# A two-layer hybrid backbone: modulation products between the layers, one indirect transfer per 128 rows, second experts by columns

## Chip, cores and metric

The kernel runs on one core of a Trainium2 chip, as one program. The metric is the device time of one execution in microseconds, the median over runs.

## The reference, cut to what matters

A latent stream (256 tokens) and a context stream (256 tokens), 1,024 wide, pass through two layers. Each layer takes six modulation rows from a product of the conditioning vector with `w_ada`; a mixer works on the normalized, modulated streams, and then a mixture of 16 experts, of which each token uses two out of one group of four. Layer 0's mixer is windowed attention beside a gated recurrence, layer 1's a gated scan beside Fourier mixing. In layer 1 only the latent stream goes on, so its experts see 256 tokens and layer 0's 512.

```python
for l in range(DEPTH):
    need_ctx = l < DEPTH - 1
    mod = (jax.nn.silu(c) @ w_ada[l] + b_ada[l])[:, None, :]
    mod_c = (jax.nn.silu(c_ctx) @ w_ada[l] + b_ada[l])[None, None, :]
    sh1, sc1, g1, sh2, sc2, g2 = jnp.split(mod, 6, axis=-1)
    ...
    h = layer_norm_affine(DEEPNORM_ALPHA * h + g1 * m, ln_g[l, 0], ln_b[l, 0])
    u = modulate(layer_norm(h), sh2, sc2)
    ...
    h = layer_norm_affine(DEEPNORM_ALPHA * h + g2 * y, ln_g[l, 1], ln_b[l, 1])

def moe(t, w_router, b_router, w1, w3, w2):
    ...
    for e in range(N_EXPERTS):
        h = jax.nn.silu(t @ w1[e]) * (t @ w3[e])
        y = y + gates[:, e:e + 1] * (h @ w2[e])
```

## The kernel before

The program runs in five stages: `mixer0` (from L631), `moe` for layer 0 (L1451 on, with `l == 0`), `mixer1` (L1083), `moe` for layer 1, and a tail (L1918 on) with the last norm. Within a stage a planner lays out each engine's order ahead of time from estimated durations, and it interleaves steps of neighbouring experts; where `in_order` (L149) is called, the order written in the code holds for the engines named. The second `moe` calls it for PE, ACT and DVE.

Precision: a product in the mixers is made of three passes over fp32r halves. `split` (L351) makes a high half by a copy on ACT (L353) and a low half by a subtraction on DVE (L355); `split_w` (L359) does it for a weight, with one buffer for the low half `wl`. The experts' products are plain fp32.

Modulation: `w_ada` comes in 12 column parts `j` of 512 per layer. `ada_load` (L244) fetches one as two tiles of 1 MB, `ada_part` (L248) does 16 matmuls with it (L254). `ada_row` (L271) adds the bias row, which it fetches into the one tile `bz` on POOL's queue (L274), and broadcasts the result over the partitions for either stream (L281); `ada_col` (L260) copies it on ACT (L262) and transposes it into columns with eight small matmuls (L265). In `mixer0` a generator `fill0` (L656) hands these steps out one by one between the projections' weights and the heads of the recurrence: rows 4 to 11 of layer 0, then eight column parts of layer 1.

Experts: `Ring` (L1421) hands out weight tiles of 1 MB from a round of slots in three pools, among them the slots `m` of `rp` and `w` of `wp`, which the mixers use for other things; six tiles make an expert, loaded on SP (L1441). `load_more` asks for tiles ahead. An expert takes its tokens in units: `cni` holds, per expert, the count in units of 32 rows, and branches (`tc.If`) on it leave out what isn't needed. In `moe` of layer 0 the tokens' rows are gathered from DRAM by indirect transfers on POOL, 64 rows each, and results scattered to `y_d` likewise (L1508). `up` (L1581, L1585) makes both up products of 64 rows in 32 matmuls, `mid` the gating on ACT and DVE (L1598, L1599), `hpose` transposes (L1605, copied on DVE at L1607), `down` (L1610, L1613) takes 16 matmuls.

In `moe` of layer 1 the rows are picked on PE: `select` (L1512, DVE) makes a one-hot matrix, `rows` (L1520, L1525) multiplies it with the normalized stream, ACT copies (L1534, L1567), `rows_T` transposes (L1541) and modulates on DVE and ACT. Experts with at most 32 rows take `up32` (L1588, L1593) and `down32` (L1617, L1621), which work on four column groups of 32 rows. `weigh` (L1817) gates the output on ACT and splits it in two halves; `seat` (L1717) makes the transposed selection, and `add` (L1730, L1735) adds the expert's rows into four accumulators of PSUM.

`large` (L1827) comes after the experts: a conditional pass over those with more rows than the main loop holds; it loads their tiles through the same ring and isn't entered with these inputs. In `mixer1`, `y_load` (L1119) fetches the experts' two results of a block of 128 tokens into a tile `yk` of the slots `m` (L1122), `block` (L1125) combines them with the residual, norms and transposes; the blocks of the latent stream (2, 3) come first and the gate's projection weights (`cols_w`, L1099, slots `w`) follow them.

The ring's slots, as the code gives them:

```python
ring.slots += [lambda sh, dt: wx.tile(sh, dt, name="wx", tag="w", bufs=nx)] * nx
ring.slots += [lambda sh, dt: rp.tile(sh, dt, name="wm", tag="m", bufs=2)] * 2
ring.slots += [lambda sh, dt: wp.tile(sh, dt, name="w", tag="w")] * NW
```

## Time and profile before

| | us |
|---|---|
| median of 3 runs | 1491.35 (1484.99 to 1494.71) |
| profiled execution, device time | 1492.23 |
| its span | 1490.4 |
| mean granted PE clock | 0.917 of full speed |
| first mixer | 0 to about 515 |
| first experts | 521 to 846 |
| from the last product of the experts to the first of the second mixer | 846 to 894 |
| second mixer and router | 894 to 1162 |
| second experts | 1162 to 1468 |
| tail | 1468 to 1490 |

The rows below come from one profiled execution. PE is the matmul engine, PEld its weight loads, DVE, ACT and POOL the vector, scalar and general engines, SPq the queue of the engine that issues most transfers. A row of the timeline gives the start, the length, the engine, the line in the kernel, the operation with its tiles (output <- inputs), the shape and the count; in brackets stands how long the engine sat idle before and what released it. Lines are those of the kernel before.

### The profile page before, as it was taken

What the parts mean: (1) busy time and instruction counts of PE and PEld (TensorE: products, weight loads), DVE (VectorE), ACT (ScalarE), POOL (GpSimd) and SP (SyncE); (2) the same over time, 40 slices, a digit from 0 to 9 for tenths busy, and PEclk for the clock granted to TensorE, in tenths of its full rate; (3) what the DMA queues carried; (4) which work ended last, traced back from release to release, by engine and by line L of the source; (5) the groups of instructions that cost most, each with busy time, mean ns of one, the idle gap of its engine ahead of it and who ended that gap; (6) DMA issues with size and microseconds to landing.
All of it is one profiled execution on the core that took longest, in us unless ns stands there. A gap on an engine that the chain in (4) does not pass through costs nothing. (4 is left out here: it accounts for less than half of the span.)

```text
span 1490.4 us, 20670 instructions
## 1 busy us (share of the span) xinstructions
PE 1231.3 (83%) x7920; PEld 753.5 (51%) x7920; DVE 663.0 (44%) x1615; ACT 412.9 (28%) x849; POOL 101.0 (7%) x135
## 2 busy tenths in 40 slices
PE   4899999988879399999999607999976787888883
PEld 2667887555659233333333207887556244444441
DVE  4432323575767712221112167645647244444444
ACT  2323223354534011111111023451231333323222
POOL 1000000110020211111101000000010000000000
PEclk9899999998969699999999857999977899999996
DMA  8465564700011799999977052421466699979831
GB/s 286 173 225 172 200 225 170 214 13 1 1 52 62 264 338 377 363 355 372 344 285 253 21 170 88 127 63 58 156 240 246 255 344 346 368 273 326 325 128 59
DMA packets 152248, 310.69 MB, mean 208 GB/s; under 512 B 7596, under 2 KB 39660, under 8 KB 152088
## 3 DMA queue, kind: packets, MB, share of 16 engines
q1 hardware_dynamic: 146320, 296.44, 56.5%
q0 software_dynamic: 4608, 8.59, 2.1%
q10 hardware_dynamic: 1160, 3.48, 0.6%
q8 instruction: 105, 1.72, 0.5%
q14 instruction: 55, 0.45, 0.1%
HBM read 303.24 MB, written 9.44 MB: 210 GB/s over the span
## 5 line engine op out<-in xcount | busy, mean ns | idle before, releaser
L372 PE MATMUL mm<-wh,uT 128*128 128x256 f32 (+2 forms) x960 | 193.7, 297 | 7.4 <-ACT uT L353 4.8
L372 PEld LDWEIGHTS mm<-wh,uT 128*128 128x128 f32 x960 | 159.0, 198 | 20.6 <-issue 9.0
L372 PE MATMUL mm<-wl,uT 128*128 128x256 f32 (+2 forms) x480 | 141.7, 296 | 4.2 <-DVE wl L355 4.2
L1585 PE MATMUL mm<-wx,xT 128*64 128x512 f32 x504 | 143.1, 600 | 1.6 <-PEq L1753 0.8
L372 PEld LDWEIGHTS mm<-wl,uT 128*128 128x128 f32 x480 | 95.0, 198 | 5.8 <-DVE wl L355 5.3
L355 DVE TENSOR_TENSOR wl<-w,wh 128x2048 fp32r<-128x2048 f32 (+3 forms) x33 | 53.8, 1646 | 71.4 <-ACT wh L353 54.2
L1599 DVE TENSOR_TENSOR hs<-hs,mm 64x512 f32<-64x512 f32 x32 | 22.1, 691 | 127.5 <-ACT hs L1598 81.3
L1585 PEld LDWEIGHTS mm<-wx,xT 128*64 128x64 f32 x504 | 44.6, 138 | 66.3 <-issue 64.5
L254 PE MATMUL mm<-w,sT 128*32 128x512 f32 x384 | 61.3, 644 | 10.9 <-DVE v L298 9.1
L353 ACT CAST wh<-w 128x2048 fp32r<-128x2048 f32 (+3 forms) x33 | 45.8, 1388 | 67.2 <-DMA w<-in_w_in_even_dram 53.3
L372 PE MATMUL mm<-uT,wh 128*128 128x512 f32 (+1 forms) x208 | 59.0, 370 | 4.9 <-ACT wh L353 4.9
L1598 ACT ACTIVATE hs<-mm 64x512 f32<-64x512 f32 x32 | 18.8, 589 | 147.0 <-PE mm L1585 97.2
L372 PE MATMUL mm<-wo,mx 128*128 128x256 f32 x384 | 52.4, 296 | 5.3 <-ACT wo L353 3.5
L1613 PE MATMUL mm<-wx,hT 128*64 128x512 f32 x192 | 54.1, 597 | 1.7 <-PEq L1796 0.9
L372 PEld LDWEIGHTS mm<-wo,mx 128*128 128x128 f32 x384 | 49.6, 202 | 6.0 <-ACT wo L353 3.8
L1585 PE MATMUL mm<-w,xT 128*64 128x512 f32 x120 | 47.0, 596 | 0.3 <-PEq L1753 0.2
L1639 DVE COPY ys<-mm 64x512 f32<-64x512 f32 x22 | 15.2, 693 | 67.6 <-ACT ys L1639 64.4
L372 PEld LDWEIGHTS mm<-uT,wh 128*128 128x128 f32 (+1 forms) x208 | 36.4, 184 | 14.0 <-ACT wh L353 5.2
L1585 PE MATMUL tr<-wx,xT 128*64 128x512 f32 x152 | 39.1, 595 | 3.2 <-PE ac L1541 2.8
L1525 PE MATMUL ac<-h,sel 128*64 128x512 f32 x104 | 28.0, 660 | 16.4 <-DVE sel L1516 16.4
L1148 PE MATMUL tr<-cst,yk 128*128 128x128 f32 x32 | 5.4, 324 | 43.4 <-ACT yk L1141 43.4
L372 PE MATMUL mm<-uT,wl 128*128 128x512 f32 (+1 forms) x104 | 37.7, 366 | 2.3 <-DVE wl L355 2.3
(468 smaller groups left out, 2304.5 us busy)
## 6 DMA issues: line engine op xcount, KB each, us to landing
w<-in_w_ada_dram SPq DMA_DIRECT2D x48, 1024.0 KB, 6.0
wx<-in_w_expert_gate_dram SPq DMA_DIRECT2D x46, 1024.0 KB, 9.3
wx<-in_w_expert_up_dram SPq DMA_DIRECT2D x44, 1024.0 KB, 8.4
wx<-in_w_expert_down_dram SPq DMA_DIRECT2D x39, 1024.0 KB, 9.0
w<-in_w_expert_down_dram SPq DMA_DIRECT2D x15, 1024.0 KB, 7.8
w<-in_w_in_even_dram SPq DMA_DIRECT2D x13, 1024.0 KB, 10.4
w<-in_w_expert_up_dram SPq DMA_DIRECT2D x12, 1024.0 KB, 8.3
wm<-in_w_expert_down_dram SPq DMA_DIRECT2D x10, 1024.0 KB
```

The source lines that it names most:

```text
L254: nc.tensor.matmul(ps[32 * g:32 * g + 32, :], sT[:, k, :], ws[k // 4][:, k % 4, :], start=k < 4, stop=k >= 4, skip_group_check=True, tile_ ...
L353: nc.scalar.copy(hi, src)
L355: nc.vector.tensor_tensor(lo, src, hi.bitcast(FP), op=OP.subtract)
L372: nc.tensor.matmul(ps, lhs(i, k), rhs(j, k), start=(k == 0 and n == 0), stop=(k == nk - 1 and n == 2))
L1148: nc.tensor.transpose(ps[:, k * 128:(k + 1) * 128], y[:, kk_ * 128:(kk_ + 1) * 128], ident)
L1525: nc.tensor.matmul(xp[i * 64:i * 64 + 64, :], sel[:, b, :], u[:, i * 512:(i + 1) * 512], start=b == 0, stop=b == len(us) - 1, skip_group_c ...
L1585: nc.tensor.matmul(hp[i * 64:i * 64 + 64, :], xT[:, k, :], ws[2 * i + k // 4][:, k % 4, :], start=k == 0, stop=k == 7, skip_group_check=Tr ...
L1598: nc.scalar.activation(hs, hp[0:64, :], AF.Silu)
L1599: nc.vector.tensor_tensor(hs, hs, hp[64:128, :], op=OP.mult)
L1613: nc.tensor.matmul(yp[n * 64:n * 64 + 64, :], hT[:, k, :], ws[4 + k // 2][:, k % 2, n * 512:(n + 1) * 512], start=k == 0, stop=k == 3, ski ...
L1639: (nc.vector.tensor_copy if n else nc.scalar.copy)(ys[:, ns], yp[rs_, :])
```

## The change

The row parts 10 and 11 of layer 0's modulation (`g2`) and the eight column parts of layer 1 leave `fill0`; they are made at the end of the first experts, ahead of `large`, and their tiles come through the ring. In the first experts one indirect transfer handles 128 rows, and the router writes its lists in that form with plain fp32 products. In the second mixer the first gate weight is asked for ahead of the latent blocks, whose y loads are issued by POOL and whose order on DVE and ACT is pinned; the two streams lie in two tiles. `moe` becomes `moe0` and `moe1`. `moe1` takes the normalized stream as two fp32r halves and makes the transposed rows of a group of four experts at once (`group`, `half_group`, `columns`), modulated as they leave PSUM; the forms for 32 rows are gone, a second unit of 64 rows has its own conditional path (`unit_up`, `unit_down`), the output is gated and scaled in one operation (`row_out`), and an add serves two experts. Its ring has 15 slots for 16.

The diff, cut:

```diff
+    def ada_load(l, j, ring=None):
         src = w_ada[l][:, j * 512:(j + 1) * 512]
-        return [load_w(src[q * 512:(q + 1) * 512, :], 4, 512) for q in range(2)], (l, j)
+        ws = []
+        for q in range(2):
+            w = ring.tile([128, 4, 512]) if ring else wp.tile([128, 4, 512], FP, name="w", tag="w")
+            nc.sync.dma_start(w, src[q * 512:(q + 1) * 512, :].rearrange("(k p) n -> p k n", p=128))
+            ws.append(w)
+        return ws, (l, j)
...
+    def ada_row(l, j, dsts, add1=0.0, col=False, ld=None):
+
+        ld = ld or ada_load(l, j)
...
-                self.io = cp.tile([64, 2, 16 * NU], I32, name="io")
+                self.io = cp.tile([128, 2, 8 * NU], I32, name="io")
...
-            for i in range(2):
-                nc.tensor.matmul(self.tps[0:64, 0:16 * NU], R[:, i], Cm[:, i].rearrange("p e j -> p (e j)"),
-                                 start=n == 0 and i == 0, stop=last and i == 1, skip_group_check=True)
+
+            for o in range(2):
+                for i in range(2):
+                    nc.tensor.matmul(self.tps[o * 64:o * 64 + 64, 0:8 * NU], R[:, i],
+                                     Cm[:, i].rearrange("p e j -> p (e j)")[:, o::2], start=n == 0 and i == 0,
+                                     stop=last and i == 1, skip_group_check=True, tile_position=(0, o * 64))
...
-            for j, t, add1 in ((4, g1, 0.0), (5, g1, 0.0), (6, sh2, 0.0), (7, sh2, 0.0), (8, sc2, 1.0), (9, sc2, 1.0),
-                               (10, g2, 0.0), (11, g2, 0.0)):
+            for j, t, add1 in ((4, g1, 0.0), (5, g1, 0.0), (6, sh2, 0.0), (7, sh2, 0.0), (8, sc2, 1.0), (9, sc2, 1.0)):
                 yield from ada_row(0, j, [(rc[r], t[:, r]) for r in range(2)], add1, j // 2 in SLOT)
-            for j in (2, 3, 0, 1, 6, 7, 8, 9):
-                ada_col(1, j)
-                yield
...
             def y_load(b):
                 yk = rp.tile([128, 2, D], FP, name="yk", tag="m", bufs=2)
                 for k in range(2):
-                    nc.sync.dma_start(yk[:, k, :], y_d[k * 512 + b * 128:k * 512 + (b + 1) * 128, :])
+                    (nc.gpsimd if b > 1 else nc.sync).dma_start(yk[:, k, :],
+                                                                y_d[k * 512 + b * 128:k * 512 + (b + 1) * 128, :])
...
+            wt = cols_w(1568, 256)
             for i in range(2):
                 nc.sync.dma_start(lnr[i], (ln_g, ln_b)[i][0, 1:2, :].to_broadcast([128, D]))
+            start = len(nc.cur_bb.bb.instructions)
             for _ in blocks(2, 3, 1):
                 pass
+            in_order(start, (mybir.EngineType.DVE, mybir.EngineType.Activation))
             row_bcast(gnb, gla_norm[0:1, :])
             ctx_ = blocks(0, 1, 2)
             for oo in (0, 256, 512):
-                wt = cols_w(1568 + oo, 256)
+                wt = cols_w(1568 + oo, 256) if oo else wt
...
+            nb = small.tile([128, 1], FP, name="nb", tag="nb")
+            nc.vector.scalar_tensor_tensor(nb, st[0], -1.0, st[1], op0=OP.mult, op1=OP.mult)
+            for i in range(2):
+                cs = slice(i * 512, i * 512 + 512)
+                u = po.tile([128, 512], FP, name="opt", tag="opt", bufs=2)
+                nc.scalar.activation(u, hb[:, cs], AF.Identity, bias=nb, scale=st[1])
+                split(uh[:, n, cs], ul[:, n, cs], u)
...
-                with tc.If(count(e, POOL) > 2):
-                    later(gather(x[64:128, :], io[:, 0, c + 1:c + 2]))
...
+                return gather(xg[n % 3], io[:, 0, e * NP:e * NP + 1])
...
-            def up32(hp, xT, ws):
-
-                zeros(hp[:, 256:512])
-                for k in range(8):
-                    for i in range(4):
-                        nc.tensor.matmul(hp[i * 32:i * 32 + 32, 0:256], xT[:, k, 0:32],
-                                         ws[i // 2 * 2 + k // 4][:, k % 4, (i % 2) * 256:(i % 2) * 256 + 256],
-                                         start=k == 0, stop=k == 7, skip_group_check=True, tile_position=(0, i * 32))
...
+            g2 = rp.tile([128, 2, D], FP, name="g2", tag="g2")
+            lds = [ada_load(0, j, ring) for j in (10, 11)] + [ada_load(1, j, ring) for j in (2, 0, 3, 1, 6, 7, 8, 9)]
+            for ld in lds[:2]:
+                for _ in ada_row(*ld[1], [(("rowc", "rowx")[r], g2[:, r]) for r in range(2)], ld=ld):
+                    pass
+            for ld in lds[2:]:
+                ada_col(*ld[1], ld)
             large()
...
+        def select(sel, e0, step, j=0):
+
+            r = r1[:, :, e0::step] if step else r1[:, :, e0:e0 + 1]
+            shp = [128, NB, r.shape[2], 64]
+            if j:
+                for b in range(NB):
+                    nc.vector.tensor_scalar(sel[:, b, 0], io1, float(64 * j), r1[:, b, e0:e0 + 1], op0=OP.add,
+                                            op1=OP.is_equal)
+            else:
+                nc.vector.tensor_tensor(sel, io1[:, None, None, :].to_broadcast(shp), r[:, :, :, None].to_broadcast(shp),
+                                        op=OP.is_equal)
+
+        def columns(ps, k, sel):
+
+            for b in range(NB):
+                for i, u in enumerate((us[b], ul[b])):
+                    nc.tensor.matmul(ps, u[:, k * 128:(k + 1) * 128], sel[:, b].rearrange("p e s -> p (e s)"),
+                                     start=b == 0 and i == 0, stop=b == NB - 1 and i == 1, skip_group_check=True)
...
+            def half_group(sel, q):
+
+                xT = e2p.tile([128, 4, 256], FP, name="xT", tag="xT", bufs=3)
+                for c in range(2):
+                    ps = bank()
+                    for i in range(2):
+                        columns(ps[:, i * 256:(i + 1) * 256], q * 4 + c * 2 + i, sel)
+                    for i in range(2):
+                        k = q * 4 + c * 2 + i
+                        s1, s0_ = cols[:, 1, 3, k, 0:1], cols[:, 1, 2, k, 0:1]
+                        o, src = xT[:, c * 2 + i, :], ps[:, i * 256:(i + 1) * 256]
+                        if i:
+                            nc.scalar.activation(o, src, AF.Identity, bias=s0_, scale=s1)
+                        else:
+                            nc.vector.tensor_scalar(o, src, s1, s0_, op0=OP.mult, op1=OP.add)
+                return xT
...
+            def group(g):
+                sel = e2p.tile([128, NB, 4, 64], FR, name="sel", tag="sel")
+                select(sel, g, 4)
+                a = half_group(sel, 0)
+                yield
+                b = half_group(sel, 1)
+                G[g] = a, b, seats(sel)
+                yield
...
+            def row_out(y, yp, e, j, n):
+
+                rs_ = slice(n * 64, n * 64 + 64)
+                nc.vector.scalar_tensor_tensor(y, yp[rs_, :], gt[rs_, j, e:e + 1], g2[rs_, n * 512:(n + 1) * 512],
+                                               op0=OP.mult, op1=OP.mult)
...
+            def unit_up(hs, e, j, ws):
+
+                sel = e2p.tile([128, NB, 1, 64], FR, name="sel2", tag="sel2")
+                select(sel, e, 0, j)
+                xp = bank()
+                for k in range(8):
+                    columns(xp[:, k * 64:(k + 1) * 64], k, sel)
...
+            nxt = None
+            for n in range(NE + 1):
+                if n < NE:
+                    e = SEQ[n]
+                    ws = W[e]
+                    nus[n] = count(e)
+                    hss[n] = hs = e2p.tile([128, 512], FP, name="hs", tag="hs", bufs=2)
+                    xa, xb, _ = G[n // 4]
+                    cs = slice(n % 4 * 64, n % 4 * 64 + 64)
+                    hp = bank()
+                    up(hp, lambda k: (xb if k > 3 else xa)[:, k % 4, cs], ws)
+                    mid(hs[0:64, :], hp)
+                    with tc.If(nus[n] > 2):
+                        unit_up(hs[64:128, :], e, 1, ws)
+                if n:
+                    hT = hpose(e2p, bank(), hss[n - 1][0:64, :], "hT")
+                if n % 2 and n > 2:
+                    add((n - 3) // 2)
+                if n < NE - 4 and n % 4 >= 2:
+                    if n % 4 == 2:
+                        nxt = group(n // 4 + 1)
+                    next(nxt)
+                if n:
+                    e = SEQ[n - 1]
+                    ws = W.pop(e)
+                    o = (n - 1) % 2 * 64
+                    y = ys[o:o + 64, :]
+                    yp = bank()
+                    down(yp, hT, ws)
+                    with tc.If(nus[n - 1] > 2):
+                        unit_down(hss[n - 1][64:128, :], e, 1, ws)
+                    if n < NE:
+                        for i in range(2):
+                            row_out(y[:, i * 512:(i + 1) * 512], yp, e, 0, i)
+                        if n % 2 == 0:
+                            parts()
+                    else:
+                        for i in range(2):
+                            row_out(y[:, i * 512:(i + 1) * 512], yp, e, 0, i)
+                            parts((slice(i * 512, i * 512 + 512),))
+                            add(n // 2 - 1, (i,))
+                    load_more(6)
```

## Rows read from the trace of the kernel before

**Rows 1.** Page, first part: busy us, share of span, instructions, by engine

```profile
PE 1231.3 (83%) x7920; PEld 753.5 (51%) x7920; DVE 663.0 (44%) x1615; ACT 412.9 (28%) x849; POOL 101.0 (7%) x135
```

**Rows 2.** Windows: stretch, length, busy per engine; PE clock, DMA share, GB/s

```profile
255.00:294.00 39.00, 34.31 (x250) 17.99 (x248) 21.42 (x50) 13.10 (x25) 6.60 (x12) 0.87 0.58 182
521.00:846.00 325.00, 308.45 (x1383) 115.89 (x1383) 63.09 (x92) 43.39 (x73) 40.12 (x44) 0.99 0.88 310
846.00:894.00 48.00, 2.04 (x10) 1.57 (x8) 27.09 (x66) 11.37 (x14) 3.42 (x4) 0.53 0.43 138
1162.00:1468.00 306.00, 248.69 (x1910) 123.56 (x1910) 135.46 (x326) 93.50 (x208) 0.00 (x0) 0.96 0.76 279
...
600.00:650.00 50.00, 46.89 (x215) 17.44 (x213) 11.92 (x18) 7.59 (x13) 6.65 (x8) 1.00 1.04 373
```

**Rows 3.** Timeline (start, length, engine, line), PE: steps of the modulation products

```profile
178.84 1.88 PE L281 MATMUL mm<-adas,cst 128*128 128x512 f32 x4
180.64 1.92 PE L254 MATMUL mm<-w,sT 128*32 128x512 f32 x16
...
266.95 1.05 PE L265 MATMUL tr<-cst,adas 128*128 128x2 f32 x8 [0.59 <-ACT adas L262]
```

**Rows 4.** Timeline, DVE: first and last of six splits of projection weights

```profile
163.80 2.29 DVE L355 TENSOR_TENSOR wl<-w,wh 128x2048 fp32r<-128x2048 f32 x1 [4.53 <-PE mm L281]
...
240.60 2.29 DVE L355 TENSOR_TENSOR wl<-w,wh 128x2048 fp32r<-128x2048 f32 x1 [4.34 <-ACT wh L353]
```

**Rows 5.** Timeline, PE and SP's queue: first experts' end to the second mixer

```profile
832.79 0.59 PE L1585 MATMUL mm<-wx,xT 128*64 128x512 f32 x1
...
844.15 1.91 PE L1613 MATMUL mm<-w,hT 128*64 128x512 f32 x8
...
859.96 2.22 SPq L1122 DMA_DIRECT2D yk<-y_d  x4
...
894.10 0.58 PE L372 MATMUL mm<-wh,uT 128*128 128x256 f32 x1 [2.67 <-ACT uT L353]
```

**Rows 6.** Page, DMA issues: count, KB each, us from issue to landing

```profile
yk<-y_d SPq DMA_DIRECT2D x8, 512.0 KB, 6.2
...
bz<-in_b_ada_dram POOLq DMA_DIRECT2D x12, 4.0 KB, 5.6
```

**Rows 7.** Timeline, PE and SP's queue: end of the second experts

```profile
1465.46 2.27 PE L1735 MATMUL mm<-wx,wT 128*128 128x512 f32 x8
...
1471.02 0.36 SPq L1922 DMA_DIRECT2D wx<-in_ln_g_dram  x1
```

**Rows 8.** Timeline, PE and DVE: output projection, steps of the second experts

```profile
1126.07 9.24 PE L372 MATMUL mm<-wo,mix 128*128 128x256 f32 x75
...
1162.37 7.09 PE L1585 MATMUL tr<-wx,xT 128*64 128x512 f32 x32 [0.46 <-ACT xT L1549]
...
1182.38 3.66 PE L1593 MATMUL tr<-wx,xT 128*32 128x256 f32 x64
...
1188.14 0.69 DVE L1607 COPY hT<-tr 128x512 f32<-128x512 f32 x1
...
1193.66 3.65 PE L1613 MATMUL tr<-wx,hT 128*64 128x512 f32 x16 [0.30 <-PEq L1780]
...
1205.97 2.19 PE L1735 MATMUL mm<-yhl,wT 128*128 128x512 f32 x8
...
1212.16 1.93 PE L1621 MATMUL tr<-w,hT 128*32 128x256 f32 x32
```

**Rows 9.** Windows, PE alone (busy, count), lines L1593, L1525, L1541 in turn

```profile
1148.00:1472.00 324.00, 40.27 (x704) 0.94 0.77 281
1148.00:1472.00 324.00, 41.13 (x144) 0.94 0.77 281
1148.00:1472.00 324.00, 18.04 (x128) 0.94 0.77 281
```

**Rows 10.** List of waits, 1154-1472: waiter, releaser, us, times, longest

```profile
PE ac L1525 <- DVE sel L1516: 16.4, 13, 2.4
```

More of the change, by code (lines that the diff above doesn't have):

```diff
@@ L1496, in bank, with count @@
             return (trt if turn[0] % 2 else act)()
+        def count(e, *engines):
+            return nc.values_load(cni[0:1, 0, e:e + 1], engines=engines,
+                                  skip_runtime_bounds_check_because="a count of at most NT tokens, for branches only")
         with ExitStack() as es:
-            e2p = pool(es, f"e4p{l}", 2)
+            e2p = pool(es, "e4p0", 2)
             def gather(t, col):
@@ L1553, in rows_Ts @@
-            def rows_Ts(xs):
-                return [rows_T(x, f"xT{i}") for i, x in enumerate(xs)]
-            def take(n):
-                e = SEQ[n]
-                nus[n] = count(e, PE)
-                sels = [select(e, j) for j in range(2)]
-                x = [fetch(sels[0])]
-                with tc.If(nus[n] > 2) as c1:
-                    xp = rows(sels[1])
-                with c1.Else():
-                    zeros(xp)
-                x.append(e2p.tile([128, 512], FP, name="x", tag="x", bufs=2))
-                tc.keep_in_program_order(nc.scalar.copy(x[1], xp))
-                return x
@@ L1676, in unit_up @@
-            def unit_up(m, e, j, ws, half=False):
-                if l == 0:
-                    xp = act()
-                    xT2 = e2p.tile([128, 8, 64], FP, name="xT2", tag="xT2", bufs=1)
-                    for k in range(8):
-                        nc.tensor.transpose(xp[:, k * 64:(k + 1) * 64], xo[m][:, k * 128:(k + 1) * 128],
-                                            ident[m * 64:m * 64 + 64, m * 64:m * 64 + 64])
-                    nc.vector.tensor_copy(xT2, xp.rearrange("p (k t) -> p k t", k=8))
-                else:
-                    xT2 = rows_T(fetch(select(e, j)), "xT0")
-                    hs2[m] = e2p.tile([128, 512], FP, name="hs", tag="hs", bufs=2)[64:128, :]
+                scatter(ys, io[:, 1, e * NP:e * NP + 1])
@@ new lines, in scatters, with unit_up @@
+                with tc.If(count(e, POOL) > 4):
+                    scatter(yo[0:64, :], io[0:64, 1, e * NP + 1:e * NP + 2])
+            def unit_up(m, ws):
+                xp = act()
+                xT2 = e2p.tile([128, 8, 64], FP, name="xT2", tag="xT2", bufs=1)
+                for k in range(8):
+                    nc.tensor.transpose(xp[:, k * 64:(k + 1) * 64], xo[m][:, k * 128:(k + 1) * 128],
+                                        ident[m * 64:m * 64 + 64, m * 64:m * 64 + 64])
+                nc.vector.tensor_copy(xT2, xp.rearrange("p (k t) -> p k t", k=8))
@@ L1730, in add @@
-            def add(n, wT):
-                for i in range(2):
-                    for b, acc in enumerate(accs):
-                        for q, y in enumerate((yhl[n // (NE - 1)][:, 0], yhl[n // (NE - 1)][:, 1])):
-                            nc.tensor.matmul(acc[i], wT[:, b * 128:(b + 1) * 128], y[:, i * 512:(i + 1) * 512],
-                                             start=n == 0 and q == 0, stop=n == NE - 1 and q == 1,
-                                             skip_group_check=True)
@@ L1739, in count @@
-            def count(e, *engines):
-                return nc.values_load(cni[0:1, 0, e:e + 1], engines=engines,
-                                      skip_runtime_bounds_check_because="a count of at most NT tokens, for branches only")
+                down(yp2, hT2, ws)
+                rows_out(yo[0:64, :], yp2)
             def first_up(n, xT, nu):
-                e = SEQ[n]
-                ws = W[e]
-                hp = [(bank if l else mmt)() for _ in range(2)]
+                ws = W[SEQ[n]]
@@ L1865, in moe @@
                 if n < NE:
-                    if l == 0:
-                        if n + 2 < NE:
-                            gathers(n + 2)
-                        if n + 1 < NE:
-                            gather3(n + 1)
-                        nus[n] = count(SEQ[n], PE, ACT, DVE)
+                    if n + 2 < NE:
+                        gathers(n + 2)
+                    if n + 1 < NE:
+                        gather3(n + 1)
+                    nus[n] = count(SEQ[n], PE, ACT, DVE)
@@ L1901, in moe @@
             last = nc.cur_bb.bb.instructions[-1]
-        return (accs, last) if l else y_d
+        return accs, last
     sr = ctx.enter_context(ExitStack())
```

501 lines of the change are left out of this document (207 added, 294 removed).

## Prediction

> **What bounds the kernel now.** I read the page's first part first: PE is busy 83% of the span [rows 1]. That share is an average, so the next view is the table of windows [rows 2]. In 255-294 PE works 34.31 of 39 us and in 521-846 (first layer's experts) 308.45 of 325: there PE sets the pace, with the DMA share at 0.88. In 846-894, between the layers, PE works 2.04 of 48 us: this stretch is a chain of latencies. In 1162-1468 (second layer's experts) PE works 248.69 of 306 and the DMA share is 0.76: neither is full, so waits between engines count. 600-650 gives the most that the transfers reach, 373 GB/s, so a tile of 1 MB costs 1.0486/0.373 = 2.8 us.
>
> The list of waits names what PE lacks in the second experts: DVE's selections (16.4 us in this one form) [rows 10]. The timeline of the seam [rows 5] reads in order: last product 844.15+1.91 = 846.06, first loads of the experts' results at 859.96, first product of the second mixer at 894.10. So from those loads to PE is a chain of 34.1 us.
>
> **1. Modulation products leave the first mixer.** One product step is 16 matmuls, 1.92 us; a row product adds 1.88 of broadcasts, a column product 1.05 of transposes [rows 3]. Two rows and eight columns move: 10 x 1.92 + 2 x 1.88 + 8 x 1.05 = 31.4 us of PE, all in stretches where PE is nearly full. Not all of it comes back. The low half of a weight (`wl`, one buffer) takes DVE 2.29 us and can't be written before the last matmul of the weight ahead; today product steps fill that hole. The splits run from 163.80 to 240.60, five periods of 15.36 us [rows 4]. Without filler a period is 2.29, the weight's 96 matmuls at 9.24/75 = 0.123 [rows 8], 11.8, and a hand-over that I estimate at 0.1: 14.2 us. Six steps x 1.15 = 7. In 255-294 about 4 of the column steps lie, 4 x 2.97 = 11.9 us; PE idles there 4.7 anyway and other work waits for DVE and ACT, so I take 9. Sum -16; ends: -8 (only the first part) and -20 (the second whole, and some of the steps before 164). SP loses the 20 loads here too; what comes next there, the output weights, is then late no more than now.
>
> **2. They go to the end of the first experts.** 20 tiles of 1 MB pass through 14 slots behind the last expert's own tiles. Slots come free as experts 14 and 15 finish, six before 15's up phase ends at 833 [rows 5], the others after; from there 14 tiles x 2.8 = 40 us: the last lands about 873, and part, copy and transposes make 877. By PE: 846 + 31.4 = 877 also. I take 879. The ends: 862, if the planner lays products among the last experts' steps; 892, if every column product waits for its copy on ACT (8 x 0.7, as DVE's copy of such a tile in [rows 8]) and the two bias rows, one buffer, wait for each other on POOL's queue (5.6 us to landing each, [rows 6]).
>
> What is queued behind them decides the price. The loads of `yk` go into a ring slot, and the ring's slots are last used inside the conditional pass for large experts. In the tail the same construction shows: last add 1465.46+2.27 = 1467.73, first load into a ring slot issued at 1471.02 [rows 7], 3.3 us later. Behind the join stand, on SP, the norm's rows, the context blocks' y loads and the mixer's weights, and on POOL the other y loads; ACT, DVE and then PE wait for these. Today that join (846+3) is covered by the last scatter's landing, and the loads go at 859.96. After, it is 879 + 3.3 = 882: +22. The first weight (`wt`, hoisted) sits in a ring slot too and lands beside the y tiles, +3 (a tile's 2.8); the fixed order on DVE takes two half-width weight splits out of the chain, -2 (2.29 for a whole one, [rows 4]). **Gap: +23**, ends +5 (products hidden, or loads not held by the join) and +37.
>
> y loads of the first two blocks move from SP to POOL, behind the conditionals that POOL joins anyway. SP's took 6.2 us, POOL's small ones 5.6 [rows 6]: nil. The Trainium skill ("DMA: Bandwidth & Descriptors", opening table and "SWDGE vs HWDGE vs iDMA") gives the GpSimd path about 1 us to the first byte against 0.6 for SP; by it the sum would be 0.4 us higher. These two rows don't show that.
>
> **3. One indirect transfer per 128 rows.** Fewer gathers and scatters in a stage that PE fills [rows 2]: nil, with the gathers two experts ahead as cover; without that cover each would hold PE for about the 6 us that the y loads take to land [rows 6]. The last scatter ends earlier, but the join is later than it: nil. The router's 16 index products in plain fp32 have 64 columns, an eighth of those of the broadcasts (1.88/4 each, [rows 3]): 16 x 0.06 = 1 us at most, left out.
>
> **4. Second experts by columns.** PE's steps now [rows 8]: up with 64 rows 7.09, with 32 rows 3.66; down 3.65 and 1.93; add 2.19 per expert. 704 matmuls of the 32-row up [rows 9] are 11 experts of 16. The other 5 are long already. All become 64-row: +11 x (3.43 + 1.72) = +56.7. Removed: row selection 41.1, transposes 18.0 [rows 9], half the adds 8 x 2.19 = 17.5: -76.6. Added: 128 column products at 0.123 = 15.7, and second halves for the two experts with over 64 rows (144 selections are 18 units of 8 [rows 9], two more than experts). So PE's busy time hardly moves; what may go is its 57 idle us, because the chain select, product, copy, transpose, modulate is walked once per four experts.
>
> Walk through PE's order. After an up, Silu, product and copy of `hT` (1188.14+0.69 against an up's end at 1186.04, less one 0.69 for the second half: 2.1 us, [rows 8]) stand before the down. Bare expert 7.09+2.1+3.65 = 12.85. With an add behind four transposes (4 x 18.04/128 = 0.6): 7.09+0.6+2.19+3.65 = 13.5. With half a group's column products behind a selection on DVE (estimated 0.8) 12.85+0.8+16 x 0.123 = 15.6. With the other half, an add and four transposes of selections 13.5+1.97+0.6 = 16.1. Expert 0: 7.1; 1: 12.85; 2 and 3: 31.7; 4 to 7 and 8 to 11: 12.85+13.5+15.6+16.1 = 58.05 each; 12 to 15, with no group left to prepare, 52.7. Sum 220.5. The tail (2.1, 3.65, gating, splitting, a half add) takes about 10. Each of the two second halves (selection, 32 small products, 7.09, 2.1, 3.65, transposes, fp32 add) I put at 20 to 25: 45. The start moves from 1162.4 to about 1165 (high and low parts of u). End: 1165+220.5+10+45 = 1440 against 1467.7, -27; a wait at starts of 0.4 per expert gives back 6. **-21**, ends -35 and -5.
>
> DMA: with 15 slots full at the first up and the other 81 tiles streaming from about 1172, 81 x 2.8 = 227 ends at 1399: ahead of PE, but little, so a slower stream belongs to the ends.
>
> **Sum** against the profiled execution (1492.23, span 1490.4; the median of the runs is 1491.35, 0.9 lower): 1492 - 16 + 23 - 21 = **1478**.
>
> **Rivals.** *Seam stays short* (products spread under the last experts, or the y loads not held): gap +5, 1492-16+5-21 = 1460. For it: DMA share 0.88 leaves some room; against it: 14 of 20 tiles can't start before 833, and the tail's row shows the join. *Products run one after another* with copies and bias rows exposed: gap +35, 1490. For it: one `bz`, and PE has nothing else to do there; against it: a step's copy can lie under the next step's product.
>
> *Other side: the lost short form.* If PE's waits in the second experts stay (they are 57 us), dropping the 32-row form and adding two second halves make that stage end at +8 instead of -21: 1492-16+23+8 = 1507. It decides once 29 of the 57 idle us remain beside those walked. For it: 11 of 16 experts double their products. Here the Trainium skill ("TensorEngine Tiling (Array Packing)", "Theoretical Speedup") speaks against the change: up to 4x for 32 columns against 2x for 64, and these rows agree, 3.66 against 7.09; by it alone, with nothing else removed, the stage would take 56.7 us more. Against it: the removed steps are worth as much. *Transfers bound the second experts:* at their present 279 GB/s a tile is 3.76 us, 81 of them end at 1172+305 = 1477, the last down and the tail 14 later, +23 against 1467.7: 1492-16+23+23 = 1522.
>
> **How the numbers follow.** Chances: forecast 0.42 (1468 to 1488), short seam 0.20, serial products 0.20, lost short form 0.14, transfers 0.04. A bit under 1% (15 us) is what a measurement of this kernel tells from no change: bounds 1476 and 1506. Faster: the short seam and just under half of the forecast, 0.40; slower: the last two, 0.18; within: the rest of the forecast and the serial case, 0.42. The range 1454 to 1505 leaves out the better tail of the short seam and the upper half of the lost short form.
>
> **What would show it.** First mixer: first product of attention some 7 us earlier, splits of `wl` 14.2 us apart. Seam: first product of the second mixer about 894-16+23 = 901, y loads issued 3 us after the last modulation matmul (if they go earlier, the join is not what holds them). Second experts: 32 up matmuls in 7.1 us for every expert, first up to last add about 275 us (305 before); if it is 300, the waits stayed. If the stage before 846 shrinks by less than 8 us, the first term is wrong.

## The result, and the profile after

The changed kernel takes 1507.66 us (median of 4 runs, 1507.02 to 1512.63) against 1489.76 for the kernel before beside it: 1.0118 of the time, 95% interval 1.0091 to 1.0146. It is slower by some 18 us where 12 faster was forecast, and outside the range. A later control of six runs gave 1514.62 (1506.0 to 1521.28): single runs of this kernel spread by about 1%, and its two medians lie 7 us apart, so a difference between totals is good to some 7 us and the stages of the profiles tell more.

The profiled execution took 1507.34 us, its span (first to last instruction) 1505.3. PE is as busy a share of the span as before, and again the windows have to say where; all windows below have the columns of [rows 2]. The page's first part for the changed kernel:

```profile
PE 1248.2 (83%) x7293; PEld 756.6 (50%) x7293; DVE 605.6 (40%) x1408; ACT 353.1 (23%) x691; POOL 94.2 (6%) x126
```

Windows of the changed kernel: early recurrence of the first mixer, the moved products, the seam behind them, the second experts:

```profile
250.00:285.00 35.00, 30.64 (x171) 19.79 (x172) 23.06 (x57) 12.93 (x36) 4.28 (x8) 0.56 0.00 0
840.00:882.00 42.00, 30.95 (x220) 13.35 (x216) 3.39 (x11) 7.07 (x12) 2.12 (x3) 0.96 0.56 207
882.00:936.00 54.00, 4.61 (x18) 3.45 (x18) 37.85 (x88) 12.70 (x16) 3.70 (x6) 0.51 0.38 128
1192.00:1484.00 292.00, 254.25 (x1207) 112.22 (x1204) 72.54 (x114) 28.85 (x42) 0.00 (x0) 0.96 0.79 293
```

Four things are to be seen. The products take 42 us of which PE works 31. Behind them 54 us pass with PE all but idle, where 48 did before [rows 2]. The second experts take 14 us less than before, not more. And in the first window PE is 87% busy while its granted clock is 0.56, so most of it passes at 1.2 GHz, the lower of the clock's two levels (the other is 2.4).

From marks in the timelines (first and last matmuls of a kind), stage by stage, for the profiled executions of the two kernels and of the experiments that carry the argument (us):

| | before | changed | products home (e1) | no join (e3) | not serial (e5) | short form too (e7) |
|---|---|---|---|---|---|---|
| first expert product at | 525.2 | 516.7 | 528.6 | 515.1 | 517.6 | 527.8 |
| last expert product of layer 0 at | 846.1 | 838.6 | 849.4 | 836.0 | 838.6 | 849.3 |
| from there to the last modulation product | - | 43.0 | - | 52.0 | 30.0 | - |
| ... to the first y load | 13.9 | 48.0 | 10.9 | 34.2 | 35.2 | 10.8 |
| ... to the second router's last product | 294.5 | 329.4 | 294.0 | 317.6 | 318.2 | 291.5 |
| from there to the first up product | 21.9 | 24.4 | 24.5 | 24.4 | 24.5 | 24.5 |
| first up to last add | 305.4 | 291.3 | 291.4 | 294.3 | 291.3 | 258.7 |
| from there to the span's end | 22.7 | 21.6 | 21.9 | 21.8 | 22.0 | 20.0 |

Changed against before: -7.5 up to the experts' end, +34.9 over the seam and the second mixer, +2.5, -14.1, -1.1. That is +14.7 of the 14.9 between the spans.

The seam itself, PE in the changed kernel (timeline; L259, L270 and L286 are L254, L265 and L281 of before):

```profile
836.65 1.92 PE L1492 MATMUL mm<-w,hT 128*64 128x512 f32 x8
838.50 1.92 PE L259 MATMUL mm<-w,sT 128*32 128x512 f32 x16
841.54 1.95 PE L286 MATMUL mm<-adas,cst 128*128 128x512 f32 x4 [1.12 <-DVE adas L281]
...
848.92 3.46 PE L286 MATMUL mm<-adas,cst 128*128 128x512 f32 x4 [3.57 <-DVE adas L281]
...
858.55 1.05 PE L270 MATMUL tr<-cst,adas 128*128 128x2 f32 x8 [0.71 <-ACT adas L267]
...
880.56 1.05 PE L270 MATMUL tr<-cst,adas 128*128 128x2 f32 x8 [0.76 <-ACT adas L267]
917.05 1.97 PE L1152 MATMUL tr<-cst,yk 128*128 128x128 f32 x8 [35.44 <-ACT yk L1145]
```

Step after step PE waits: 1.12 and 3.57 ahead of the two row products' broadcasts (the second for its bias row, the first line below), then 0.7 to 0.8 in every column product for ACT's copy. POOL and SP's queue, with the loads behind the products:

```profile
842.91 0.61 POOL L279 DMA_DIRECT2D bz<-in_b_ada_dram  x1 [0.98 <-DMA xg<-u_d,io]
...
885.14 0.36 SPq L1179 DMA_DIRECT2D lnr<-in_ln_g_dram  x1
...
886.59 2.14 POOL L1125 DMA_DIRECT2D yk<-y_d  x4 [0.31 <-issue]
```

The last transposes end at 881.6, the first load on SP goes 3.5 later, the y loads at 886.6 against 859.96 before [rows 5].

### The profile page after: what moved, and what is told of

Same layout as the page of the kernel before. It is cut to its first block, busy times and chain, and to the rows that moved or that the text cites. A ratio compares the mean times of both kernels' runs of the same rounds, so it can differ in the third digit from the quotient of the medians.

```text
span 1505.3 us, 18933 instructions
## 1 busy us (share of the span) xinstructions
PE 1248.2 (83%) x7293; PEld 756.6 (50%) x7293; DVE 605.6 (40%) x1408; ACT 353.1 (23%) x691; POOL 94.2 (6%) x126
## 5 line engine op out<-in xcount | busy, mean ns | idle before, releaser
L377 PE MATMUL mm<-wh,uT 128*128 128x256 f32 (+2 forms) x960 | 187.8, 292 | 3.2 <-ACT wh L358 2.1
L377 PEld LDWEIGHTS mm<-wh,uT 128*128 128x128 f32 x960 | 155.1, 194 | 11.3 <-issue 5.7
L377 PE MATMUL mm<-wl,uT 128*128 128x256 f32 (+2 forms) x480 | 139.3, 292 | 11.8 <-DVE wl L360 11.8
L377 PEld LDWEIGHTS mm<-wl,uT 128*128 128x128 f32 x480 | 92.9, 194 | 14.0 <-DVE wl L360 13.4
L1485 PE MATMUL ac<-wx,xT 128*64 128x512 f32 x216 | 60.3, 595 | 3.7 <-PEq L1873 2.1
L1485 PE MATMUL tr<-wx,xT 128*64 128x512 f32 x200 | 51.7, 618 | 5.2 <-PEq L1873 2.3
L259 PE MATMUL mm<-w,sT 128*32 128x512 f32 x264 | 41.1, 644 | 8.4 <-DVE sT L218 7.0
L1485 PE MATMUL ac<-w,xT 128*64 128x512 f32 x88 | 41.2, 622 | 1.5 <-PEq L1873 0.8
```

Of the source, the lines that this page charges most:

```text
L259: nc.tensor.matmul(ps[32 * g:32 * g + 32, :], sT[:, k, :], ws[k // 4][:, k % 4, :], start=k < 4, stop=k >= 4, skip_group_check=True, tile_ ...
L377: nc.tensor.matmul(ps, lhs(i, k), rhs(j, k), start=(k == 0 and n == 0), stop=(k == nk - 1 and n == 2))
L1485: nc.tensor.matmul(hp[i * 64:i * 64 + 64, :], xT(k), ws[2 * i + k // 4][:, k % 4, :], start=k == 0, stop=k == 7, skip_group_check=True, ti ...
```

## The experiments

**e1: the products back home.** The change without its first part:

```diff
+                               (10, g2, 0.0), (11, g2, 0.0)):
...
+            for j in (2, 3, 0, 1, 6, 7, 8, 9):
+                ada_col(1, j)
+                yield
...
-            lds = [ada_load(0, j, ring) for j in (10, 11)] + [ada_load(1, j, ring) for j in (2, 0, 3, 1, 6, 7, 8, 9)]
```

> The changed kernel with the ten modulation products back in the first mixer, where they were; all else as changed. Theory S (the move of the products is what costs, its price the longer seam): the first experts end about 8 us later than in the changed kernel (846), the first product of the second mixer comes within 50 to 55 us of that end instead of 97, and the total is near 1507 + 8 - 35 = 1480, 0.6% under the kernel before, carried by the second experts. Rival M (the seam is long because of the pinned order and the loads by POOL, not because of the products): the seam stays near 85 to 97 us and the total is 1500 or more.

1483.89 us, 0.9962 of before (0.9939 to 0.9985), and 24 under the changed kernel. The seam is back at before's length (294.0 against 294.5 to the router), with the pinned order and POOL's loads still in; the first gate product comes 59.7 us after the experts, 48.0 before, about what the pin costs by e2, and it is made up by the router. So the move alone makes the seam longer, by 35.5 us, and gives back 8 to 14 in the first mixer (first expert product 528.6 against 514.5 to 520.4 in seven profiles of the changed kernel's first mixer; against before's own 525.2 it is 5 to 11).

**e2: no pinned order.**

```diff
-            in_order(start, (mybir.EngineType.DVE, mybir.EngineType.Activation))
```

> The changed kernel without the pinned order of the latent blocks on DVE and ACT in the second mixer. Theory P: the pin makes ACT's half of the first block's transposed rows wait for the second block's norm (first transposes 917.1, their rows on ACT at 932.9), so without it the first gate product comes 10 to 14 us earlier; part of it was given back within the mixer already, so the first up product of the second experts and the total are 4 to 10 us earlier, near 1500. Rival: the second block bounds the stage anyway; the first product is earlier, but the second experts start within 2 us of the changed kernel's, total 1505 to 1509.

1506.31: the rival. The first gate product comes 86.0 us after the experts instead of 97.0, but the router's last product 327.1 after them instead of 329.4. What the pin does can be seen in ACT's timeline of the changed kernel:

```profile
915.75 1.24 ACT L1145 ACTIVATE yk<-hx,nb,rs 128x1024 f32<-128x1024 f32 x1 [12.57 <-DVE nb L1144]
...
931.79 1.24 ACT L1145 ACTIVATE yk<-hx,nb,rs 128x1024 f32<-128x1024 f32 x1 [7.84 <-DVE nb L1144]
932.94 1.48 ACT L1158 ACTIVATE xT<-tr,cols 128x128 f32<-128x128 f32 x4
```

The first block's transposes were done by 919, and their rows on ACT wait until 932.94 behind the second block's norm. It costs the first product 11 us and the stage 2. Where the other 9 are lost again wasn't followed.

**e3: no join.**

```diff
             for ld in lds[2:]:
                 ada_col(*ld[1], ld)
-            large()
```

> The changed kernel without the conditional pass for large experts after the first experts (it isn't entered with these inputs, so no work that runs is left out; a kernel for all inputs would need it). Theory J (the y loads wait for the join of that pass, which PE reaches only after the last modulation product): the y loads of the latent blocks go when the last product has read their ring slots, 862 to 870 instead of 886.6, and the first gate product comes 12 to 20 us earlier; total 1490 to 1497. Rival: they wait for something else after the products (their slots, the column results), and the y loads move by less than 5 us; total 1503 to 1508.

1498.82 (ratio 1.0056), 9 under the changed kernel. POOL's timeline:

```profile
870.17 1.11 POOL L1125 DMA_DIRECT2D yk<-y_d  x2 [17.13 <-PE mm L259]
```

The y loads now go 34.2 us after the experts instead of 48.0, released by the product that last read their ring slots, although the products end later (52.0 after, beside the y loads). To the router it is 11.8 us less; the total is 2 us over what was expected. The join holds the loads, as forecast.

**e4 and e12: four products more in the early recurrence.**

```diff
                 for n in range(4):
                     next(fl, None)
+                    dd = cst[:, None, 0:512].to_broadcast([128, 4, 512])
+                    ada_col(1, (2, 0, 3, 1)[n], ([dd, dd], (1, 0)))
                     yield
```

> The changed kernel with four more column products in the first mixer's recurrence, where four of the moved ones stood; they work on constants, load nothing, and their result is overwritten. Theory C (without that filler PE's granted clock falls: 0.5 from 255 to 280 in the changed kernel, 0.8 to 1.0 before): the clock there comes back to 0.8 or more, the first experts start no later than in the changed kernel, and the total is between 1500 and 1508. Rival W (PE's work is what counts there): four products of 3 us are added, the first experts start 8 to 12 us later, total 1515 to 1520.

The clock came back and the first expert product was 2.8 us earlier (513.9), yet the time was 1515.86, as the rival had it, and the profile has 3.4 us more between the first and the second experts and 3.5 more in the second, whose instructions are the same. So it was run again (e12) beside the changed kernel itself as a control (e11).

> The changed kernel itself, as the control beside the next run: 1507 to 1509, first experts from about 517, PE's granted clock near 0.56 in 250 to 285.

> The fourth experiment again, with its control on the same chip (four more column products on constants in the early recurrence). Its first run started the first experts 2.8 us earlier, as theory C has it, and yet took 8 us longer in all, 1515.9. If that excess was of that run or of its chip, the total is now within 4 us of the control's. If it is of the kernel (the later stages, whose instructions are the same, run slower after a busier first mixer), it is again 6 to 10 us above the control, with the excess after the first experts.

The control gave 1514.62 (1506.0 to 1521.28), over the 1507 to 1509 expected, its first expert product at 520.4, its clock in the window 0.55; e12 gave 1517.11 (1509.43 to 1521.46): 2.5 apart, inside both spreads, so the excess of the first run isn't shown to be the kernel's. The four products are 12 us of PE work by [rows 3]. First expert product: 513.9 in one profile, 526.6 in the other, against 516.7 and 520.4 without them. The same window in the kernel before, in e4 and in e12, to be read beside the 0.56 above:

```profile
250.00:285.00 35.00, 30.31 (x242) 19.22 (x240) 21.34 (x49) 13.38 (x25) 6.08 (x11) 0.90 0.54 179
```

```profile
250.00:285.00 35.00, 33.10 (x266) 18.94 (x264) 22.34 (x61) 13.26 (x36) 3.71 (x8) 1.00 0.00 1
```

```profile
250.00:285.00 35.00, 32.93 (x240) 18.92 (x241) 20.23 (x50) 11.48 (x23) 3.63 (x8) 0.87 0.00 1
```

More work in the same stretch, at over one and a half times the clock. Taken whole, from the last product of the projections to the first of the output projection, the stretch reads so in the kernel before, the changed one, e11, e4 and e12:

```profile
255.53:430.72 175.19, 148.06 (x1026) 90.48 (x1026) 111.63 (x308) 76.51 (x214) 16.08 (x32) 0.86 0.16 49
247.31:421.60 174.29, 145.12 (x930) 93.40 (x930) 110.87 (x304) 74.64 (x210) 16.28 (x32) 0.76 0.00 1
249.49:425.02 175.53, 146.91 (x931) 94.57 (x931) 110.93 (x305) 74.83 (x210) 16.35 (x32) 0.75 0.00 1
246.12:418.77 172.65, 146.37 (x1028) 91.76 (x1027) 111.40 (x309) 76.98 (x214) 15.45 (x32) 0.86 0.00 1
248.07:424.29 176.22, 149.20 (x1026) 92.55 (x1027) 111.68 (x309) 76.68 (x214) 14.96 (x32) 0.85 0.00 1
```

96 matmuls, four product steps, are in or out, and the stretch hardly changes: 172.7 to 176.2 us with them, 174.3 and 175.5 without. (In the other five profiles with the changed kernel's first mixer it is 171.1 to 175.5.) So the late start in e12's profile comes from elsewhere: its output projection took 67.4 us, the others' 60.2 to 60.5. What fills the place of the four steps is the other 930 matmuls, which run longer at the lower clock. One group of 112 of them in these stretches, before, changed and e4 (busy us, mean ns of one):

```profile
L958 PE MATMUL mm<-hx,kh 64*128 64x128 f32 x112 | 25.8, 356 | 3.2 <-DVE S L963 2.3 <-DVE S L961 0.6 <-ACT P L858 0.3
L961 PE MATMUL mm<-hx,kh 64*128 64x128 f32 x112 | 28.4, 405 | 2.4 <-DVE S L966 1.3 <-DVE S L964 0.9 <-ACT P L861 0.2
L961 PE MATMUL mm<-hx,kh 64*128 64x128 f32 x112 | 25.6, 359 | 2.4 <-DVE S L966 1.3 <-DVE S L964 0.7 <-ACT P L861 0.3
```

The same product takes 356 ns with the fillers, 405 without, and 359 with fillers that load nothing and whose result nobody reads.

**e5: the products not one after another.**

```diff
+            sb = first_half(0)
+            for i in range(1, 10):
+                nxt_ = first_half(i)
+                second_half(i - 1, sb)
+                sb = nxt_
+            second_half(9, sb)
+            in_order(start, (PE, ACT))
```

`first_half` is the 16 matmuls and the copy (or the add of a bias row fetched long before), `second_half` the broadcasts or transposes.

> The changed kernel with the products between the layers no longer one after another: both bias rows fetched before the experts into two tiles, and each step's 16 matmuls issued ahead of the transposes of the step before, so that ACT's copies and the bias wait have cover on PE. Theory Q (half of what the forecast missed at the seam is this serial order: 43 us from the last expert product to the last modulation product where 33 were forecast): the products end 32 to 36 us after the experts, y loads and first up product come 7 to 11 us earlier, total 1496 to 1501. Rival D (the tiles' transfers bound them, so the products can't end earlier): 40 us or more, total 1504 to 1509.

1496.90 (ratio 1.0042). PE's timeline:

```profile
838.56 1.92 PE L259 MATMUL mm<-w,sT 128*32 128x512 f32 x16
840.30 1.90 PE L259 MATMUL mm<-wx,sT 128*32 128x512 f32 x16
842.13 1.99 PE L1703 MATMUL mm<-adas,cst 128*128 128x512 f32 x4
844.04 1.93 PE L259 MATMUL mm<-wx,sT 128*32 128x512 f32 x16
...
866.69 1.95 PE L1708 MATMUL tr<-cst,adas 128*128 128x2 f32 x16
```

No wait is left in it: 30.0 us from the experts to the last transposes, where the sum of steps is 31.4. So the transfers didn't bound them, and 13 of the 43 us were the price of the order (10.7 of them stand as waits in the changed kernel's timeline). To the router it is 11.2 us less.

**e6: no second units in the second experts.**

```diff
-                    nus[n] = count(e)
...
-                    with tc.If(nus[n] > 2):
-                        unit_up(hs[64:128, :], e, 1, ws)
...
-                    with tc.If(nus[n - 1] > 2):
-                        unit_down(hss[n - 1][64:128, :], e, 1, ws)
```

> The changed kernel without the two conditional second units of the second experts, with their branches and count loads: the rows beyond 64 of two experts are left out of the result. In the changed kernel first up to last add takes 291.3 us; the two units take about 47 there by its timeline. Theory B (each expert's two conditionals hold PE about 0.7 ahead of the up and 0.3 ahead of the transposes): 291.3 - 47 - 16 = 228 us, and the gap ahead of each up falls from 0.7 to under 0.2. Rival (those gaps are waits for DVE or for weights): 291.3 - 47 = 244, the gaps stay.

1453.96; first up to last add takes 236.4 us, between the two. Rows of the changed kernel and then of e6, PE, one expert without a group to prepare:

```profile
1200.18 7.09 PE L1485 MATMUL tr<-wx,xT 128*64 128x512 f32 x32 [0.71 <-PEq L1856]
1207.42 0.43 PE L1476 MATMUL ac<-cst,hs 64*128 64x64 f32 x4 [0.15 <-PEq L1856]
1209.18 3.65 PE L1492 MATMUL tr<-wx,hT 128*64 128x512 f32 x16 [1.32 <-issue]
```

```profile
1210.38 0.46 PE L1476 MATMUL ac<-cst,hs 64*128 64x64 f32 x4
1212.35 3.65 PE L1492 MATMUL tr<-wx,hT 128*64 128x512 f32 x16 [1.50 <-DVE hT L1478]
1215.83 0.59 PE L1485 MATMUL ac<-wm,xT 128*64 128x512 f32 x1
...
1222.80 0.46 PE L1476 MATMUL tr<-cst,hs 64*128 64x64 f32 x4
```

L1856 is the unit's conditional. Without it the gaps ahead of the up (the next one follows the down at 1215.83) and of the transposes are gone, but the down waits longer for DVE's copy (1.50, where 1.32 stood). 291.3 - 236.4 = 54.9, of which some 47 are the two units by the timeline, so the branches of 16 experts, with the loads of their counts, are worth 8 us, half of what was put on them. Part of their time lay beside that wait.

**e7: the short form back.** e1, and in the second experts

```diff
-                    up(hp, lambda k: (xb if k > 3 else xa)[:, k % 4, cs], ws)
+                    xTn = lambda k: (xb if k > 3 else xa)[:, k % 4, cs]
+                    with tc.If(nPs[n] > 1) as c0:
+                        up(hp, xTn, ws)
+                    with c0.Else():
+                        up32(hp, xTn, ws)
```

likewise for the down and for the rows on DVE; the gates move into the split of the outputs.

> The changed kernel with the products back in the first mixer (as in the first experiment, 1483.9) and with the 32-row products back in the second experts, each behind a conditional on PE, the gates moved into the split of the outputs. Theory L (what the change lost in the second experts is the short form; the column form doesn't need it gone): 11 experts save 3.43 + 1.72 each, all 16 pay two more branches of 0.3 to 0.7, so the stage falls from 291 us to 255 to 270 and the total to 1448 to 1463. Rival T (the transfers bound the stage by then: 81 tiles at 2.8 us after the first up): no shorter than 275, total 1466 to 1472. Rival U (branches eat the gain): 285 or more, total 1478 or more.

1447.96, 0.9725 of before (0.9678 to 0.9771): theory L. The stage falls to 258.7 us. PE's short up, and the window in which the transfers run full:

```profile
1174.15 3.66 PE L1777 MATMUL tr<-wx,xT 128*32 128x256 f32 x64
```

```profile
1200.00:1240.00 40.00, 33.75 (x312) 17.71 (x311) 13.65 (x27) 6.33 (x9) 0.00 (x0) 1.00 1.04 391
```

**e8: four steps moved into the attention.** e1 with the last four column steps between weights handed out beside the attention instead.

```diff
-                    next(fl, None)
+                    if off not in (2304, 2816):
+                        next(fl, None)
...
-                for _ in attention():
+                for n, _ in enumerate(attention()):
                     yield
+                    if n % 3 == 2:
+                        next(fl, None)
```

> The products back in the first mixer as in the first experiment (1483.9, first experts from 528.6), but four of the column products that stood between the last projection weights moved into the attention, whose PE has idle time and a falling clock. Theory C+W (between weights a step costs 1.2 us, since the wait for a weight's low half hides the rest; beside the attention it costs nothing, since it keeps the clock up): the first experts start 3 to 6 us earlier, total 1478 to 1481. Rival: beside the attention it costs its 3 us of PE, the start is 5 to 8 us later, total 1489 to 1492.

1494.66: the rival, its total 3 us over. The projections end 6.4 us earlier (a step between weights costs 1.6), but the first expert product is at 535.4 against 528.6. From the projections' end that is 13.1 us for four steps: there a step costs its 3 us and more.

**e9: four real products kept in the early recurrence.**

```diff
                     next(fl, None)
+                    ada_col(1, 6 + n)
...
-ada_load(1, j, ring) for j in (2, 0, 3, 1, 6, 7, 8, 9)]
+ada_load(1, j, ring) for j in (2, 0, 3, 1)]
```

> The changed kernel with four of the ten moved products (the second norm's columns of the second layer) done in the first mixer's recurrence, with their real loads, and six left between the layers. Theory C (in the early recurrence a product step is free, since it keeps PE's clock up) with the serial price of 3.67 us a column at the seam: the first experts start within 3 us of the changed kernel's, the seam shrinks by 4 x 3.67 = 15 us, total 1489 to 1495. Rival W (each step costs its 3 us of PE there): the first experts start 9 to 12 us later, total 1500 to 1506.

1494.54, 20 under the control beside it. First expert product 520.8 (control 520.4); the last modulation product 24.2 us after the experts instead of 44.3, the router 314.2 instead of 332.1: 18 us off the seam. That the first experts start no later is in part luck: this profile's projections ended at 245.6, the control's at 249.5, and from there to the output projection it takes 180.1 against 175.5:

```profile
245.61:425.70 180.09, 152.76 (x1026) 93.51 (x1026) 111.50 (x308) 76.82 (x214) 15.86 (x32) 0.83 0.15 48
```

So four real products, with their loads, cost some 5 of their 12 us there in this one profile; the four on constants cost 1 or nothing by the rows above.

**e10: the move at its best.** The changed kernel with e5's order, without the join, with e7's short form.

```diff
             in_order(start, (PE, ACT))
-            large()
```

> The changed kernel with the products left between the layers but issued without serial waits, without the join of the pass for large experts ahead of the y loads (that pass isn't entered with these inputs), and with the short form back in the second experts. If the parts add: 1507.7 - 11 (serial waits) - 11.7 (join) - 32.7 (short form) = 1452, beside 1448 with the products at home, so moving them is worth about nothing even then. Rival (the two seam terms overlap, since both bring the same y loads forward and the y loads then wait for the products' ring slots): only one of the two counts, total 1460 to 1466.

1448.57, 0.9716 of before (0.9677 to 0.9755): the parts add. The y loads go 17.1 us after the experts, while the products still run. It equals e7 (1447.96): even with both waits gone, the move is worth nothing. The first expert product comes 8.2 us earlier than in e7 (519.6), and experts to router take 302.6 against 291.5.

## Why the prediction was wrong, step by step

**First mixer, -16 forecast, -8.5 measured (-7.5 at the experts' end).** The first half was right: the projections end 8.2 us earlier (7 forecast), and the splits of the low halves run from 162.50 to 233.42, five periods of 14.2 (14.2 forecast). The second half, 9 us in the recurrence, is the step that failed: from the projections' end to the first expert product it is 269.6 us before and 269.4 after. PE's work there went, and its clock went with it: 0.56 instead of 0.90 in 250 to 285, 0.76 instead of 0.86 over the whole stretch. PE's busy time fell by 3 us and not by 12, because the same products take longer (405 ns for 356), and its idle time rose by 2. "PE idles there 4.7 anyway and other work waits" asked what PE does, and not at which clock the rest would run. That the clock is the cause is shown by e4: work that has no other use, put back in the same place, brings back the clock (0.86) and the time of a product (359). By the Trainium skill ("TensorE: Matmul & The Clock Gate", Part 1) the throttled state is the default and activity releases it; the windows agree in direction, 0.56 without the steps and 0.87 to 1.00 with them. By the forecast's own sign (a shrinkage of less than 8 us before 846) this term was wrong.

**Seam, +23 forecast, +34.9 measured.** The mechanism was right: the y loads wait for the join, and the join for the last product; e3 shows it. The term that was too small is the products' end, 43 us after the experts and not 33; from there to the y loads it was 5.0 and not 3.3. The forecast had both parts of it, copies exposed on ACT and two bias rows on one tile, as the rival "products run one after another", gap +35, at a chance of 0.20; e5 takes the waits away and gets 11.2 us back. "A step's copy can lie under the next step's product" was an argument about what can be; the order that was laid out doesn't do it. Its chain from the y loads to the first product was also 34.1 in the forecast and 49 in the profile, but 11 of that is the pin's, and all but 2 of the 11 is given back before the router (e2).

**One transfer per 128 rows, POOL's loads: nil forecast.** First expert product to last takes 320.9 before and 321.9 after, and e1's seam is that of before. Right.

**Second experts, -24 and +3 at the start forecast, -14.1 and +2.5 measured.** The walk held for its steps and for the two second units (47 against 45). Mis-sized was what stands between steps. From one up to the next a bare expert takes 13.4 us in the timeline (12.85 forecast), one with an add 14.2 (13.5), and one that begins a group 17.6 (15.6), three times: there PE waits 1.7 for the selection on DVE, put at 0.8, and from the transposes' end at 1221.43 to the down at 1226.17 it takes 4.7 instead of 2.8. The stage is 16 us over the walk (275.5), of which the sum had set 6 aside; its sign of "about 275" left even these out. The branches were not the larger part: 8 us by e6, with their counts, against those 6.

**The rivals.** The time came out at that of the lost short form, 1507, but by coincidence: that rival has the second experts 8 us longer, and they became 14 shorter. Yet the form was worth having. From before to e7, with the column form and the short form together, the stage gains 46.7 us (305.4 to 258.7), and the changed kernel gives 32.6 of them back (291.3). The forecast set +56.7 against -76.6 and took the balance; it didn't ask whether the two had to come together. Transfers didn't bound the stage. With the short form they run full in one stretch of it (share 1.04, 391 GB/s in 1200 to 1240), but rival T's 275 us at least did not come, and PE's waits for them add up to 2.6 us in the whole stage.

So -11.6 in the second experts and -7.5 up to the first experts' end stand against +34.9: the move of the products decides. Without it e1 is 0.4% faster than before, e7 2.7%. All three terms came out on the slow side, the first two at or near the slow ends that the forecast gave them (-8, +37), the third on its way there (-5). With all three ends the sum is 1516; the range stopped at 1505.

## What to carry to other kernels

Before work is moved out of a full stretch, ask at what clock the rest will run without it, and before it is moved into an idle one, ask who is queued behind it: here the loads waited for a conditional pass that wasn't even entered. Compare stretches between marks of the work itself and not between fixed times: e9's and e12's starts mislead until the stretch before them is taken out. Steps of product, copy, transpose written one after another pay each copy, unless the order is written so that the next product comes first. When a change swaps one form for another, price the parts apart: the gain (columns) didn't need the loss (no short form).

## What the runs showed of the hardware

PE can be 87% busy over 35 us at a granted clock of 0.56, and four more product steps in the same stretch raise it to 1.00 or 0.87 (0.81 with real ones, e9's window). Over the whole recurrence these steps were free or nearly so. A conditional that isn't taken leaves a gap of 0.71 ahead of PE's next product. The Trainium skill ("Advanced Engine Details and Errata", Control Flow Timing) gives a compare-and-branch about 0.11 us; the measurement decides, though it is of a conditional with the load of its count, and only 8 us came back when 32 of them were removed, 0.25 each.
